# A tile of its own for the last phase's scaled x, and low halves of the second input projection read back from DRAM

## The chip, the core and the metric

The kernel runs on one core of one Trainium2 chip. The metric is the device time of one execution in microseconds (us). Three runs of the kernel before took 2285.0, 2285.44 and 2281.86 us; their median is 2285.0 us. One further execution was profiled, and the views quoted below come from it.

## What is computed

One layer of a hybrid decoder for two groups of requests that share the weights: a prompt of 1024 tokens and 8 sample tokens, model width 1024. Cut to its core:

```python
h = x + 0.5 * rmsnorm(swiglu(rmsnorm(x, n_ffn1_pre), gate1, up1, down1), n_ffn1_post)   # d_ff 2816
u = rmsnorm(h, n_mix_pre)
proj = u @ w_in                      # 1024 x 3328: 26 column tiles of 128
q, k, v = split(proj[..., :1536])    # group A: differential attention, 4 heads
pb = proj[..., 1536:]                # group B: RWKV-7, 8 heads of 64
ya = rmsnorm(attend(rope(q), rope(k), v), subln) * (1 - lam_init)
yb, state, shift = rwkv7_time_mix(pb, prev_shift, state0)
h = h + rmsnorm(concat(ya, yb) @ w_out, n_mix_post)
h = h + 0.5 * rmsnorm(swiglu(rmsnorm(h, n_ffn2_pre), gate2, up2, down2), n_ffn2_post)
```

The sample tokens attend over a paged cache of 512 past positions and carry a given RWKV state. Outputs are h for both groups, the new keys and values, the RWKV states and the last projected row.

## The kernel before

**Two halves, four phases.** Tokens lie along the free axis, features along the partitions. The 1032 tokens are cut into two halves: half 0 holds prompt tokens 0 to 511 and the 8 samples, half 1 prompt tokens 512 to 1023, as far as the first feed-forward goes. The feed-forward runs as phases 0 and 1 (first FFN of each half) and 2 and 3 (second FFN of each half; in phase 3 the samples lead). Each phase works on two column chunks, c = 0 and 1, of 256 or 264 tokens; phases 1 and 2 mostly use both at once (512 columns). Between them lie the input projection (`s_project`, half 0 and half 1), RWKV jobs (`s_job`), attention, and the output projection (`s_out`).

**Three matmuls for one.** Weights and activations in float32 are split into a high part, rounded to the fast matmul type, and a low part, the rest: `high = round(x)`, `low = x - high`. Each product is three matmuls that add up in PSUM: high x high, high x low, low x high (`mm3`). One weight tile of the input projection is 128 x 1024 numbers, 512 KB, for the high as for the low part. It gives 8 x 3 = 24 matmuls for each chunk.

**Where the low part comes from.** `split` (line 602) casts the raw tile to the high part on ScalarE, and then either subtracts on VectorE or GpSimd (`low`; `choose` takes the engine that is expected to be free first) or, where `kept` names a place in DRAM, reads the low part that an earlier use of the same weight wrote there. `first` marks the use that writes:

```python
if kept is not None and not first:
    self.aside(mine, kept)                   # read the low part from DRAM
...
    self.nc.scalar.copy(h[:, t], raw[:, t])
    if kept is None or first:
        self.low(l[:, t], raw[:, t], h[:, t].bitcast(F32))
if first and kept is not None:
    self.aside(kept, mine)                   # write it to DRAM
```

`LOWS` says for which weights this is done: before the change for the second FFN (`1`: DRAM tiles Ld, Lg) and the output projection (`"out"`: Lo). `K.Li`, the place for the input projection's 26 tiles, exists but is not used. `aside` issues these transfers on SyncE's DMA queue (SP), where nearly all other transfers are issued too, in order.

**The input projection.** `s_project` (line 1446) takes its 26 column tiles m in an order `ms`: 24, 25, 16, 12, 20, and so on; in half 1 the rest are 17, 13, 21, 18, 14, 22, 19, 15, 23, then 0 to 11. `s_linear` (line 655) loads each raw tile (two buffers in turn, lraw for even places and LT for odd ones in half 1), waits until the tile two places earlier has been used, and calls `split` into the weight tile of that earlier one. Half 0 works in units of 256 or 264 columns, half 1 from the third tile on in units of 512. Half 1's vector norm, `s_tail` of phase 1, comes just before its projection; its steps are called tail in the trace.

**Phase 3's input.** `s_pre(3)` (line 1214) scales the second residual by the row norm (`t = src * rstd`), eight tiles for each chunk, and splits each into the high and low matmul operands with `pair`: a ScalarE activation and a VectorE scalar_tensor_tensor, both of which read t. t lies in the pool tile `sq`, of which there are two, used in turn. The same two are used by the square sums at the end of a phase (`down(..., tail)` in `s_trunk`, through `square_sum`, line 755; in the trace trunk_sq, which are added to trunk_acc), by `s_tail`, and by `s_combine`. In the trace the scaled x is pre_sq, and the operands of phase 3 are pre_T.

**The tile dreg.** `dreg` is one large pool tile (128 x 4160 floats) with many tenants: activations of phase 1, the sample tokens' attention and RWKV step, half 1's attention (low parts of q and k, mix_dreg), and last, from `s_combine(3)` on, four sums of blocks of phase 3's input. `s_combine` forms such sums in phases 0 and 3 for a scheme that makes seven block products do for eight (`seven`), from the eleventh (phase 0) or fifth (phase 3) tile of the FFN's width on.

**A planned order.** The program does not run in the order in which it is written. Streams (generators with a label) hand operations to a planner, which keeps a model of the engines, orders the operations of every engine, and fixes that order in the program. It runs four times; from each run it works out the latest time at which each operation may start, and these due times are the priorities of the next one. `BIAS` (line 94) adds microseconds to the due times of a stream, named by label and count: a negative number makes its operations more urgent. `comb0` is `s_combine(0)`; `job03` is the fourth stream named job0, the second RWKV job of half 1 on buffer set 0 (`s_job`, i = 2). Any edit changes the plan as a whole.

Of the kernel before, what the change touches and what calls it, by code (L numbers as in the profile page):

```python
# [22 lines left out]
P = 128  # L23
# [34 lines left out]
def const_table():  # L58
# [11 lines left out]
    for g in range(4):  # L70
        for j in range(8):
# [8 lines left out]
W_DEC = 4160  # L80
# [10 lines left out]
MARG = 0  # L91
SLACK = 0.02
PASSES = 4
BIAS = {"trunk2": 300, "outn3": -60, "outb0": 30, "pre2": -3, "tail1": -30, "lora1": -10}
SHIFT = {}
SWAP = 0
MIX = 1
SQP = 0
RESAT = 3
GROUPS = {(0, 10): [[0, 1, 2], [3, 4], [5, 6, 7], [8, 9]], (3, 6): [[0, 1, 2], [3], [4, 5]],  # L100
          (0, 8): [[0, 1, 2], [3, 4], [5], [6, 7]], (0, 6): [[0, 1, 2], [3], [4, 5]], (3, 4): [[0, 1], [2, 3]], (3, 8): [[0, 1, 2], [3, 4], [5], [6, 7]]}
LOWS = (1, "out")
STARVE = 1
HUNGER = 0.1
RB = "dec"
# [107 lines left out]
class Kern:  # L213
# [99 lines left out]
    def put(self, eng, op, fn, a, k):  # L313
# [14 lines left out]
        if o.late is not None:  # L328
            o.late += BIAS.get(st.part, 0) + sum(d for a, b, d in self.shift.get(st.part, ()) if a <= o.key[1] < b)
        self.price(o, op, a, k, outs[0], ins)  # L330
# [468 lines left out]
    def stats(self, src, rb, tmp=("sqs", 1), **kw):  # L799

        for k in range(KT):
            if SQP:
                self.square_sum(rb, src[k], k, self.ps2()[:, :rb.shape[-1]], engines=("vector",))
            else:
                self.square_sum(rb, src[k], k, self.tmp(*tmp, rb.shape[-1]), **kw)
        self.rstd(rb)
# [64 lines left out]
    def s_weights(self):  # L871
# [3 lines left out]
        for ph in range(4):  # L875
# [4 lines left out]
            for n, (kind, f, m0) in enumerate(seq):  # L880
# [26 lines left out]
                kept = None  # L907
                if ph // 2 in LOWS and (kind == "down" or f < FAST[3 * (ph // 2)]):
                    kept = self.Ld[ph // 2][grp[0]:grp[-1] + 1, :, m0 * P:m0 * P + nm].rearrange("q p m -> p q m") if kind == "down" else \
# [304 lines left out]
    def s_pre(self, ph):  # L1214

        half = ph % 2
        if ph > 1:
            yield ("wait", ("outw", half))
        for c, (_, n) in enumerate(CHUNKS[ph]):
            yield ("wait", ("stage", ph, c))  # L1220
            if ph:
                yield ("wait", ("stats", ph, c))
            if c == 0:
                tiles = self.two(half)
                x = self.x[ph] = self.parts(ph, *tiles)
                self.xt[ph] = [t.rearrange("p (k t) -> p k t", t=520) for t in tiles]
            for k in range(KT):
                src = self.staged[c]
                if ph:

                    t = self.tmp("sq", 2, n) if ph == 3 else src[k]
                    self.either("tensor_tensor", t, src[k], self.own[c][2][:, :n], ALU.mult)
                    src = {k: t}
                for step in self.pair(k, src, f"n_ffn{1 + ph // 2}_pre", x[c]):
                    step()
                if k % 4 == 3:
                    yield
            self.signal(("x", ph, c))
            yield
        self.signal(("staged", ph))  # L1240
# [205 lines left out]
    def s_project(self, half):  # L1446

        nc = self.nc
        places = None
        for c in range(2):  # L1450
            yield ("wait", ("prb", half, c))
        if half:
            yield ("wait", ("outw", 0))
        else:
            yield ("wait", ("loaded", 1, "up", LEAD - 1, None))
            places = ("w0", "w1"), [("used", 1, kind, LEAD - 1, None) for kind in ("gate", "up")]

        job = [16, 12, 20]
        ms = [24, 25] + job
        ms = ms + [m + i for i in range(1, 4) for m in job] + list(range(12)) if half else \  # L1460
            ms + [m + 1 for m in job] + list(range(8)) + [m + i for i in range(2, 4) for m in job] + list(range(8, 12))

        def out(i, c, ps):
            o, n = SPANS[half][c]
            po = (self.rb if i % 2 else self.E)[:, o:o + n]
            nc.vector.tensor_tensor(po, ps, self.prb[:, o:o + n], ALU.mult)
            nc.sync.dma_start(self.PT[ms[i]][:, FIRST[half] + o:FIRST[half] + o + n], po)
            if c:
                self.signal(("done", half, ms[i]))

        units = [(i, c) for i in range(len(ms)) for c in ((2,) if half and i > 1 else range(2))]
        if half:
            units[:4] = [(0, 0), (1, 0), (0, 1), (1, 1)]
        yield from self.linear(("in", half), [self.column(self.I["w_in"], m) for m in ms], units, None, out, places,
                               [(self.Li[m], half == 0) for m in ms] if "in" in LOWS else None)
        self.signal(f"proj{half}")

    def s_out(self, half):
# [48 lines left out]
        if half:  # L1527
            yield ("wait", "states")
        yield from self.linear(("out", half), src, units, px, out, None, [(self.Lo[i % KT], half == 0) for i in range(len(src))] if "out" in LOWS else None)
        self.signal(("outw", half))  # L1530
# [1117 lines left out]
```

## Time and profile before

| | us |
|---|---|
| median of 3 runs | 2285.0 |
| lowest and highest run | 2281.86, 2285.44 |
| the profiled execution | 2287.04 |
| its span in the profile | 2284.6 |
| TensorE (PE) busy in the span | 2223.3 |
| VectorE (DVE), ScalarE (ACT), GpSimd (POOL) busy | 1537.3, 1098.8, 986.9 |
| moved by DMA | 343.15 MB |

The profiled execution took 2.04 us more than the median, and 2.4 us of its time lie outside the span. In a row of the timeline stand the start and the length of a run of like instructions, what they write and read, how many they are, and in brackets how long the engine was idle before and what released it. A matmul's length holds its pipelining, so the rate is read from a run of many. PEclk is TensorE's granted clock as a share of full speed. All operations are issued through one helper, so every row has line 320; the tiles' names tell them apart.

### The profile page before, as it was taken

How to read it: one execution, taken by the hardware profiler on the slowest of the kernel's cores; microseconds unless marked ns; L12 is line 12 of the kernel's file. 1: busy time of each engine (PE TensorE's matmuls, PEld its weight loads, DVE VectorE, ACT ScalarE, POOL GpSimd, SP SyncE). 2: the span in 40 equal slices, each digit the busy share in tenths (PEclk: the TensorE clock that was granted, in tenths of full speed). 3: DMA queues.
4: the chain of work that ended last, by engine and by line, in shares of the span. 5: the costliest groups of instructions: out<-in, count | busy, mean ns of one | idle time of the engine just before them, and what ended most of it. 6: DMA issues, size and time to landing. Idle time of an engine off the chain costs nothing.

```text
span 2284.6 us, 42790 instructions
## 1 busy us (share of the span) xinstructions
PE 2223.3 (97%) x15857; PEld 1981.1 (87%) x15857; DVE 1537.3 (67%) x3550; ACT 1098.8 (48%) x2256; POOL 986.9 (43%) x819
## 2 busy tenths in 40 slices
PE   7999999999999999999999999999999998999998
PEld 7999999799887778888877877777788888999998
DVE  5477888745766776568766466664676365778776
ACT  5443443635454366344562155543576555544444
POOL 3344555524333675456443124333434354544443
PEclk9999999999999999999999999999999999999999
DMA  6423334354433685655668753334636857434543
GB/s 203 135 84 94 110 93 131 102 148 140 113 107 104 184 244 174 211 177 151 178 205 213 193 146 111 106 86 115 199 112 172 276 165 240 148 114 126 148 139 112
DMA packets 476295, 343.15 MB, mean 150 GB/s; under 512 B 82457, under 2 KB 424061, under 8 KB 476088
## 3 DMA queue, kind: packets, MB, share of 16 engines
q1 hardware_dynamic: 475480, 338.82, 50.6%
q8 instruction: 125, 2.05, 0.4%
q0 software_dynamic: 320, 1.08, 0.1%
q14 instruction: 82, 0.67, 0.1%
q10 hardware_dynamic: 288, 0.52, 0.1%
HBM read 278.98 MB, written 61.38 MB: 149 GB/s over the span
## 4 chain that ended last, share of the span: by engine, by line
PE 77%; DVE 6%; ACT 6%; DMA 5%; issue 3%; POOL 2%; SPq 1%; DVEq 0%; ACTq 0%; POOLq 0%
PE trunk_m L320 44%; PE proj_m L320 12%; PE trunk_aux L320 7%; PE job_aux L320 4%; PE out_m L320 2%; PE outb_m L320 2%; PE attn_m L320 2%; PE attn_aux L320 1%; SPq L320 1%; ACT wts_w L320 1%; ACT mix_T L320 1%; DMA wts_raw<-in_ffn_gate_dram 1%; PE job_dec L320 1%; DMA lin_w<-Lo 1%; POOL wts_w L320 1%
## 5 line engine op out<-in xcount | busy, mean ns | idle before, releaser
L320 POOL TENSOR_TENSOR wts_w<-wts_raw,wts_w 128x1024 fp32r<-128x1024 f32 (+2 forms) x161 | 310.8, 1938 | 351.3 <-ACT wts_w L320 303.5
L320 PE MATMUL trunk_m<-trunk_xl,wts_w 128*128 128x256 f32 (+2 forms) x2700 | 456.5, 320 | 4.4 <-DVE trunk_xl L320 3.7
L320 PE MATMUL trunk_m<-pre_X,wts_w 128*128 128x512 f32 (+3 forms) x2400 | 439.9, 334 | 4.9 <-DVE pre_X L320 2.0
L320 PEld LDWEIGHTS trunk_m<-trunk_xl,wts_w 128*128 128x128 f32 x2700 | 381.4, 188 | 40.7 <-DVE trunk_xl L320 5.8
L320 PEld LDWEIGHTS trunk_m<-pre_X,wts_w 128*128 128x128 f32 x2400 | 351.3, 190 | 44.8 <-issue 3.7
L320 PE MATMUL trunk_m<-pre_T,wts_w 128*128 128x512 f32 (+3 forms) x1848 | 365.0, 348 | 6.5 <-DVE trunk_xl L320 2.7
L320 ACT CAST wts_w<-wts_raw 128x1024 fp32r<-128x1024 f32 (+2 forms) x293 | 244.2, 848 | 241.3 <-PE trunk_m L320 167.2
L320 PEld LDWEIGHTS trunk_m<-pre_T,wts_w 128*128 128x128 f32 x1848 | 288.1, 191 | 44.3 <-issue 3.9
L320 DVE TENSOR_TENSOR trunk_xl<-trunk_xl,trunk_m 128x256 f32<-128x256 f32 (+2 forms) x351 | 165.9, 491 | 57.7 <-PE trunk_m L320 56.4
L320 POOL TENSOR_TENSOR trunk_xl<-trunk_t,trunk_xl 128x512 fp32r<-128x512 f32 (+3 forms) x88 | 94.7, 1078 | 169.2 <-ACT trunk_xl L320 168.8
L320 PE MATMUL proj_m<-tail_xl,lin_w 128*128 128x256 f32 (+1 forms) x1248 | 166.5, 288 | 0.0
L320 PEld LDWEIGHTS proj_m<-tail_xl,lin_w 128*128 128x128 f32 x1248 | 153.9, 188 | 6.9 <-issue 5.1
L320 PE MATMUL proj_m<-tail_T,lin_w 128*128 128x512 f32 (+1 forms) x672 | 150.4, 380 | 3.0 <-DVE tail_T L320 1.9
L320 PEld LDWEIGHTS proj_m<-tail_T,lin_w 128*128 128x128 f32 x672 | 120.6, 188 | 31.0 <-DVE tail_T L320 3.0
L320 DVE TENSOR_TENSOR wts_w<-wts_raw,wts_w 128x1024 fp32r<-128x1024 f32 (+2 forms) x102 | 109.6, 1075 | 34.7 <-ACT wts_w L320 32.4
L320 POOL TENSOR_TENSOR lin_w<-lin_raw,lin_w 128x1024 fp32r<-128x1024 f32 x21 | 51.6, 2457 | 110.6 <-ACT lin_w L320 106.7
L320 ACT CAST wts_w<-wts_lraw 128x512 fp32r<-128x512 f32 x94 | 55.7, 619 | 72.0 <-DMA wts_lraw<-in_ffn_down_dram 35.0
L320 POOL TENSOR_TENSOR wts_w<-wts_lraw,wts_w 128x512 fp32r<-128x512 f32 x43 | 60.0, 1398 | 45.2 <-ACT wts_w L320 41.9
L320 PE MATMUL trunk_aux<-trunk_xl,wts_w 128*128 128x256 f32 (+1 forms) x516 | 71.7, 283 | 0.0
L320 DVE TENSOR_TENSOR trunk_t<-trunk_g,trunk_m 128x512 f32<-128x512 f32 (+2 forms) x75 | 41.9, 559 | 44.1 <-PE trunk_m L320 41.7
L320 PE MATMUL trunk_m<-comb_T,wts_w 128*128 128x260 f32 x540 | 69.4, 282 | 0.0
L320 ACT CAST wts_w<-wts_dec 128x512 fp32r<-128x512 f32 x30 | 17.6, 587 | 103.7 <-DVE wts_dec L320 102.0
(647 smaller groups left out, 4263.8 us busy)
## 6 DMA issues: line engine op xcount, KB each, us to landing
wts_raw<-in_ffn_gate_dram SPq DMA_DIRECT2D x88, 512.0 KB
wts_raw<-in_ffn_up_dram SPq DMA_DIRECT2D x58, 512.0 KB
wts_raw<-in_ffn_down_dram SPq DMA_DIRECT2D x56, 384.0 KB
wts_raw<-in_ffn_down_dram SPq DMA_DIRECT2D x29, 512.0 KB
lin_raw<-in_w_in_dram SPq DMA_DIRECT2D x26, 512.0 KB
wts_w<-Ld SPq DMA_DIRECT2D x22, 512.0 KB
mix_T<-PT SPq DMA_DIRECT2D x37, 256.0 KB
Ld<-wts_w SPq DMA_DIRECT2D x24, 384.0 KB
```

Source lines behind the costliest of these rows:

```text
L320: o = Op(eng, lambda: fn(*a, **k), st)
```

## The change

Four edits. In phase 3 the scaled x gets 16 separate slices of `dreg`, a new tenant of it, in place of the two `sq` tiles in turn. The input projection's low parts go through DRAM where m is odd (`ODD = 1`; 13 of 26 tiles): half 0 subtracts as before and writes the low part to `Li`, half 1 reads it and does not subtract. An even m is left as it was, in both halves. Two entries are added to `BIAS`: comb0 -60 and job03 +60. The edit of `stats` and `SQP` alone does nothing, since `SQP` is empty as it was 0.

```diff
-BIAS = {"trunk2": 300, "outn3": -60, "outb0": 30, "pre2": -3, "tail1": -30, "lora1": -10}
+BIAS = {"trunk2": 300, "outn3": -60, "outb0": 30, "pre2": -3, "tail1": -30, "lora1": -10, "comb0": -60, "job03": 60}
-SQP = 0
+SQP = ()
+ODD = 1
-LOWS = (1, "out")
+LOWS = (1, "in", "out")
@@ def stats
-            if SQP:
+            if SQP and tmp[0] in SQP:
@@ def s_pre
                 self.xt[ph] = [t.rearrange("p (k t) -> p k t", t=520) for t in tiles]
+                scaled = self.T(self.pool, [P, W_DEC], "dreg") if ph == 3 else None
...
-                    t = self.tmp("sq", 2, n) if ph == 3 else src[k]
+                    t = scaled[:, 2112 * c + n * k:2112 * c + n * k + n] if ph == 3 else src[k]
@@ def s_project
-                               [(self.Li[m], half == 0) for m in ms] if "in" in LOWS else None)
+                               [(self.Li[m], half == 0) if not ODD or m % 2 else () for m in ms] if "in" in LOWS else None)
```

## The prediction

> **What bounds the kernel now.** I read the page first, then the busy time by stage, then what TensorE waited for in the stages that the change touches, and last the timeline around those waits.
>
> ```profile
> span 2284.6 us, 42790 instructions
> PE 2223.3 (97%) x15857; PEld 1981.1 (87%) x15857; DVE 1537.3 (67%) x3550; ACT 1098.8 (48%) x2256; POOL 986.9 (43%) x819
> ```
>
> TensorE is busy for 97% of the span. The change leaves every matmul in place, so it can only act on the 2284.6 - 2223.3 = 61.3 us in which TensorE waits, and on the clock that is lost around waits. The stages (span; busy time of PE, PEld, DVE, ACT, POOL; granted clock, DMA share, GB/s) are: half 0's projection, the passage from phase 1 to half 1's projection, that projection, half 1's output projection, and the passage from phase 2 to 3:
>
> ```profile
> 456.00:680.00 224.00, 222.70 (x2046) 205.11 (x2046) 135.95 (x443) 99.09 (x183) 72.96 (x57) 1.00 0.44 128
> 1120.00:1185.00 65.00, 58.77 (x372) 52.44 (x372) 51.81 (x92) 42.56 (x78) 33.94 (x39) 0.97 0.72 216
> 1185.00:1322.00 137.00, 137.00 (x598) 110.02 (x598) 74.57 (x106) 34.51 (x39) 29.71 (x14) 1.00 0.76 197
> 1760.00:1855.00 95.00, 92.98 (x597) 83.22 (x596) 36.41 (x66) 47.40 (x81) 33.83 (x37) 1.00 0.82 258
> 1855.00:1910.00 55.00, 49.10 (x348) 44.77 (x347) 41.89 (x74) 35.22 (x66) 30.57 (x33) 1.00 0.43 129
> ```
>
> Where the low parts are to be read, 1185 to 1322, TensorE has no idle time at all. Time is lost in the two passages: 65 - 58.77 = 6.2 us and 55 - 49.10 = 5.9 us. From 1855 to 1960 TensorE waited for (total, times, longest):
>
> ```profile
> PE rows_cb L320 <- ACT rows_X L320: 2.2, 2, 1.5
> PE last_aux L320 <- ACT trunk_xl L320: 2.1, 1, 2.1
> PE trunk_m L320 <- ACT trunk_sq L320: 1.9, 1, 1.9
> PE trunk_m L320 <- DVE trunk_xl L320: 0.8, 1, 0.8
> ```
>
> **Part 1: the scaled x.** No operation is added or removed; 16 multiplications write other slices. What goes is the turn-taking on two tiles, with phase 2's closing square sums in the same queue for them. Rows of VectorE, ScalarE, GpSimd and TensorE:
>
> ```profile
> 1885.33 0.75 DVE L320 TENSOR_TENSOR trunk_xl<-trunk_xl,trunk_m 128x256 f32<-128x256 f32 x2
> 1897.50 0.43 DVE L320 TENSOR_TENSOR trunk_acc<-trunk_acc,trunk_sq 128x256 f32<-128x256 f32 x1 [0.62 <-POOL trunk_acc L320]
> ...
> 1889.86 0.51 ACT L320 ACTIVATE pre_T<-pre_sq,setup_cols 128x256 fp32r<-128x256 f32 x1 [0.31 <-POOL pre_sq L320]
> 1890.27 0.40 ACT L320 ACTIVATE trunk_sq<-trunk_xl 128x256 f32<-128x256 f32 x1
> ...
> 1890.75 2.40 POOL L320 TENSOR_TENSOR trunk_acc<-trunk_acc,trunk_sq 128x256 f32<-128x256 f32 x3 [0.93 <-ACT trunk_sq L320]
> ...
> 1884.70 0.59 ACT L320 COPY rows_X<-rows_cb 128x512 f32<-128x512 f32 x1
> 1885.34 0.66 PE L320 MATMUL rows_cb<-init_ident,outb_T 128*128 128x128 f32 x4 [0.68 <-ACT rows_X L320]
> ...
> 1898.40 5.02 PE L320 MATMUL trunk_m<-trunk_xl,wts_w 128*128 128x256 f32 x35 [0.82 <-DVE trunk_xl L320]
> 1908.01 6.09 PE L320 MATMUL trunk_m<-pre_T,wts_w 128*128 128x264 f32 x48 [1.88 <-ACT trunk_sq L320]
> ```
>
> The second result of phase 2's close was there at 1885.33 + 0.75 = 1886.1, yet its square began at 1890.27, right behind the last step that reads the scaled x: 4.2 us late. GpSimd's additions start late with it, VectorE waits at 1897.50 for them, the eviction queued behind that addition comes late, and TensorE waits 0.82 us at 1898.40. Meanwhile phase 3's operands, for whose sake the squares stood back, are first used at 1908.01, some 17 us after they were done at 1890.4. With places of their own the scaled x need no longer be read before the squares can be written. I take as gained the 0.82 us, the 1.88 us at 1908.01 (ScalarE works off squares there) and the 0.68 us at 1885.34, where a copy to the rows is queued among the scaled x's steps: **-3.4 us**. Bounds: nothing, if ScalarE's order alone held the square back, and -3.4 - 2.1 = -5.5 us, if the wait for trunk_xl in the list goes too. The new tenant of dreg makes nobody wait: what held it before is half 1's attention, over when the output projection starts at about 1760, and what follows on it, the block sums, waits for all of the scaled x already.
>
> **Part 2: 13 subtractions less, 13 reads more.** Tile 25, second in the order, is odd. Its subtraction lies on the chain of waits (start, length) before half 1's projection:
>
> ```profile
> 1131.53 0.18 DVE lin_w L320
> 1131.71 0.94 issue
> 1132.65 1.26 DVE trunk_xl L320 x3
> 1133.92 0.74 POOL trunk_xl L320
> 1134.67 4.23 DMA tail_hres<-res
> ...
> 1131.49 3.10 PE L320 MATMUL trunk_m<-pre_X,wts_w 128*128 128x256 f32 x24
> 1153.04 4.05 PE L320 MATMUL trunk_m<-pre_X,wts_w 128*128 128x256 f32 x21
> ```
>
> Without it the chain moves up by 0.18 + 0.94 = 1.1 us. The waits in this passage also cost clock: 21 matmuls at 4.05 / 21 = 193 ns against 129 ns (3.10 / 24) earlier, 21 x 0.064 = 1.3 us, with 0.97 granted over the stage. I take both: **-2.5 us**, bounds 0 and -2.5. By the Trainium skill (TensorE: Matmul & The Clock Gate, What's actually happening) the clock falls after an idle window of about 3.4 us. No single wait here is that long and the clock fell all the same, so the trace doesn't bear this out in that form. By the rule the short waits would have cost no clock, and this term would be -1.1 us.
>
> The other 12 odd tiles are among the 24 wide ones. In the stage 1185 to 1322:
>
> ```profile
> L320 PE MATMUL proj_m<-tail_T,lin_w 128*128 128x512 f32 x575 | 135.1, 395 | 0.0
> L320 DVE TENSOR_TENSOR lin_w<-lin_LT,lin_w 128x1024 fp32r<-128x1024 f32 x9 | 11.5, 1274 | 0.8 <-ACT lin_w L320 0.8
> L320 POOL TENSOR_TENSOR lin_w<-lin_lraw,lin_w 128x1024 fp32r<-128x1024 f32 x6 | 14.5, 2418 | 56.4 <-ACT lin_w L320 41.0 <-DMA mix_T<-PT 12.5 <-DMA decb_dreg<-Dd 2.9
> ```
>
> 12 subtractions at 1.27 us (VectorE) to 2.42 us (GpSimd) are 15 to 29 us of engine time, and TensorE waited 0.0 us for any of it: this is worth **0**. The price is on the other side. A read can be issued once the tile two places back is used; until its low part is needed TensorE has one tile, 24 x 135.1 / 575 = 5.64 us, and the two matmuls on the high part, 0.47 us: 6.1 us of cover. The like reads of the output projection:
>
> ```profile
> L320 PE MATMUL outb_m<-outb_T,lin_w 128*128 128x264 f32 (+1 forms) x384 | 48.9, 284 | 2.0 <-DMA lin_w<-Lo 1.9
> ...
> 1812.85 7.93 DMA lin_w<-Lo
> 1823.73 5.62 DMA lin_w<-Lo
> ```
>
> Those that set the end took 5.62 to 7.93 us. Per read that is between no wait and 7.93 - 6.1 = 1.8 us, for 12 between 0 and 22 us. I take what 16 such reads cost there, 1.9 us, or 0.12 each: **+1.5 us** for 13. A tile there lasts only 24 x 48.9 / 384 = 3.1 us, with other matmuls put in between; here it lasts longer. While such a read waits on SP for its slot, everything behind it waits as well: the projection's results on their way to PT, and the loads of the sample tokens' RWKV step; TensorE waits for neither in this stage. The reads bring 12 x 0.524 MB in 137 us, 46 GB/s, on 197; with the share per GB/s of the output projection's stage (0.82 at 258) the DMA share rises from 0.76 to about 0.91. The Trainium skill (DMA: Bandwidth & Descriptors, Latency and other measured facts) puts an access to DRAM at 0.2 us on average and 2 us at high load; that speaks against the middle I chose, and for reads near the 7.93 us. This is a rival below.
>
> Half 0 writes 13 low parts, 30 GB/s more on 128. The slot is needed again two tiles later, and the write starts before its tile is used, so it has two tiles' time. The nearest row is the first output projection, which writes 8 low parts in shorter tiles:
>
> ```profile
> L320 PE MATMUL out_m<-out_X,lin_w 128*128 128x256 f32 x384 | 46.6, 281 | 0.0
> ```
>
> TensorE waited 0.0 us there: **0**. Were the cover gone, one write late by the 1.8 us above, once, would be the price.
>
> **Part 3: the two biases.** Phase 0's block sums are ready long before they are used; rows of VectorE and TensorE:
>
> ```profile
> 161.97 0.96 DVE L320 TENSOR_TENSOR comb_T<-comb_sq,comb_T 128x260 fp32r<-128x260 f32 x1
> ...
> 195.28 1.60 PE L320 MATMUL trunk_m<-comb_dreg,wts_w 128*128 128x260 f32 x12
> ```
>
> That is 32 us of slack, so comb0 earlier by up to 60 us is worth **0**; it might cost the 1 us that one displaced subtraction lasts. job03 acts between 1322 and 1600, where TensorE waited for jobs:
>
> ```profile
> PE job_aux L320 <- ACT mix_T L320: 2.3, 7, 0.6
> PE job_aux L320 <- DVE mix_T L320: 1.2, 4, 0.5
> PE job_aux L320 <- DVE job_hres L320: 1.1, 1, 1.1
> ```
>
> Together 4.6 us. One of four jobs is moved, and against its partner on the other buffer set, so that one's short matmuls can fall into the other's gaps. Bounds are all of it gone and as much again, -4.6 and +4.6. I take a quarter, **-1.2 us**.
>
> **The sum:** -3.4 - 2.5 + 1.5 - 1.2 = -5.6 us. Against the profiled execution's 2287.04 us that is 2281.4; this execution lay 2.04 us above the median of the runs, 2285.0, and on the scale of the runs the forecast is **2279.4 us**.
>
> **The rivals.** (a) *The reads come late and TensorE becomes bound by them.* Speaking for it: no idle time in the stage now, and a share of 0.91 where 0.82 gave landings up to 7.93 us. Against it: in the outputs' stage TensorE lost only 1.9 us. It decides from a landing of 6.1 us on. At half of the way to 7.93, 0.9 us a read, 12 reads cost 11 us in place of 1.5: -5.6 + 9.5 = +3.9, 2289 us; at the full 1.8 us, 22 us, 2300 us. I put it at 2291. (b) *More goes than I count.* Part 1 at its bound (-5.5), the jobs at theirs (-4.6), tile 25 in full and the reads hidden: -5.5 - 4.6 - 2.5 = -12.6, 2272 us. For it: the passages hold 12.1 us of waits. Against it: other waits are often next in line. (c) *It is hidden anyway.* The square was late because ScalarE was full, the chain before the projection is met by its load of the residual, and only the +1.5 us of the reads remains, or nothing: 2285 to 2286.5. For it: the 17 us of slack show that phase 3's input as such is not on the path. Against it: the 0.82 us follow step by step from the late square. (d) *The new plan as a whole* moves waits that no part touches; of the 61.3 us in the span I can't say which, so this widens the range only.
>
> **How the numbers follow.** Chances: forecast 0.46, with its own range 2276 to 2283; (a) 0.25; (b) 0.19; (c) 0.10. About 0.2%, 4.6 us, is what a measurement of this kernel can tell from no change: faster means under 2280.4, slower over 2289.6. Of the forecast some three quarters (0.36) and all of (b) are faster: 0.55. Of (a) most and a little of (d) are slower: 0.24. The rest, 0.21, is the same. The range runs from 2266 (b, with half as much again for the plan) to 2295 (a, between its half and its full price).
>
> **What would show it.** Part 1 is right if phase 2's second square starts within about 1 us of its input and TensorE's waits between 1880 and 1910 shrink by 3 us; wrong if the square still follows the last scaled x. Part 2 is right if half 1's projection runs 575 wide matmuls in about 135 us with waits for Li under 2 us in all, and VectorE's step before the tail's chain is gone; a list of waits of proj_m for lin_w<-Li of 5 us or more would be rival (a). comb0 is right if the first block product starts without a wait. The forecast fails if the reads land later than 6.1 us, or if waits arise in stages that no part touches.

## The result and the profile after

The changed kernel took 2297.2 us (median of 4 runs, 2292.7 to 2299.8) and the kernel before, on the same chip, 2283.4 us (4 runs). The ratio is 1.006, with a 95% interval of 1.0048 to 1.0073: some 13.8 us slower. The forecast was 2279.4 us with a range to 2295.

The profiled execution of the changed kernel took 2292.67 us, 4.55 under its median, and that of the kernel before 2287.04 us, 3.61 over the 2283.43 here. Of the 13.8 us the two profiles thus show only 5.6. The profiled execution of the changed kernel was the fastest of its four and had the highest granted clock of them (0.994; the others 0.993, 0.989 and 0.991); the place of the rest of the 13.8 us is in no trace. First the head of the page after:

```profile
span 2290.9 us, 42826 instructions
PE 2226.4 (97%) x15857; PEld 1983.4 (87%) x15857; DVE 1530.6 (67%) x3548; ACT 1097.0 (48%) x2256; POOL 960.1 (42%) x806
```

TensorE runs the same 15857 matmuls. It waits 2290.9 - 2226.4 = 64.5 us in place of 61.3, and its matmuls take 3.1 us longer in all. The busy time by stage, after (span; PE, PEld, DVE, ACT, POOL; granted clock, DMA share, GB/s):

```profile
456.00:680.00 224.00, 220.72 (x2041) 203.72 (x2040) 138.71 (x437) 98.73 (x183) 72.37 (x57) 1.00 0.52 157
1120.00:1185.00 65.00, 58.95 (x408) 54.48 (x407) 46.65 (x96) 41.70 (x79) 33.35 (x41) 0.95 0.66 203
1185.00:1322.00 137.00, 134.99 (x586) 107.31 (x585) 66.82 (x104) 37.35 (x46) 19.32 (x11) 1.00 0.97 248
1855.00:1910.00 55.00, 51.40 (x359) 47.69 (x358) 37.86 (x62) 32.27 (x66) 30.93 (x36) 0.97 0.38 115
```

The DMA share where the low parts are read rose from 0.76 to 0.97 (I had forecast 0.91), and TensorE now idles 2.0 us there. Half 0's projection, where they are written, idles 3.3 us in place of 1.3. The passage from phase 2 to 3 idles 3.6 us in place of 5.9. None of these is 13.8 us. The largest single loss is in a stage that I had not quoted, because no part of the change touches it: the close of phase 1. The same view, first before, then after:

```profile
1082.00:1120.00 38.00, 37.80 (x256) 34.42 (x254) 29.18 (x72) 16.63 (x30) 17.82 (x11) 1.00 0.46 133
```

```profile
1082.00:1120.00 38.00, 34.16 (x184) 29.24 (x183) 27.49 (x62) 13.58 (x22) 12.65 (x8) 0.91 0.39 109
```

TensorE's idle time goes from 0.2 to 3.8 us and the granted clock from 1.00 to 0.91, another 0.09 x 38 = 3.4 us. Other stages win some of it back: from 1322 to 1760 TensorE idles 6.9 us in place of 11.0. The timeline of VectorE, SP and TensorE in phase 1's close, after:

```profile
1084.13 5.18 SPq L2527 DMA_DIRECT2D dec_dreg<-in_cache_v_dram  x3
1084.66 4.29 DVE L321 SCALAR_TENSOR_TENSOR dec_dreg<-dec_dreg 128x128 f32<-128x128 f32 x8 [0.56 <-DMA dec_dreg<-in_cache_v_dram]
1088.88 1.27 DVE L321 TENSOR_TENSOR trunk_xl<-trunk_xl,trunk_m 128x512 f32<-128x512 f32 x2
1089.61 3.05 PE L321 MATMUL trunk_m<-trunk_xl,wts_w 128*128 128x512 f32 x9 [2.85 <-DVE trunk_xl L321]
```

In the new order eight steps of the sample tokens' attention (dec_dreg) stand ahead of two evictions of the trunk on VectorE's queue. They take 4.29 us, and TensorE waits 2.85 us for the evictions. In the kernel before the evictions stand one by one between such steps, and TensorE waits for none of them by more than 0.2 us from 1082 to 1120:

```profile
1084.72 2.98 DVE L320 SCALAR_TENSOR_TENSOR dec_dreg<-dec_dreg 128x128 f32<-128x128 f32 x8
1087.63 0.67 DVE L320 TENSOR_TENSOR trunk_xl<-trunk_xl,trunk_m 128x512 f32<-128x512 f32 x1
```

In the changed kernel the clock halves at about 1091, some 1.4 us after TensorE went on. Three stretches of 7 us (columns as above):

```profile
1084.00:1091.00 7.00, 4.15 (x18) 3.03 (x18) 6.44 (x15) 1.06 (x1) 2.39 (x1) 1.00 0.63 179
1091.00:1098.00 7.00, 7.00 (x23) 5.80 (x22) 5.09 (x13) 1.05 (x1) 2.37 (x1) 0.51 0.44 135
1098.00:1105.00 7.00, 7.00 (x32) 5.67 (x31) 3.07 (x7) 2.74 (x5) 2.18 (x1) 1.00 0.35 101
```

TensorE is busy for all of the second stretch, so with the wait of 2.85 us about as much again was lost in clock, 0.49 x 7 = 3.4 us. The Trainium skill (TensorE: Matmul & The Clock Gate, What's actually happening) has the clock halved after an idle window of some 3.4 us that runs free of the kernel. The halving agrees; a wait of 2.85 us, shorter than the window, was enough here.

### The profile page after: what moved, and what is told of

Read it like the earlier page. It is cut to its first block, busy times and chain, and to the rows that moved or that the text cites. A ratio compares the mean times of both kernels' runs of the same rounds, so it can differ in the third digit from the quotient of the medians.

```text
span 2290.9 us, 42826 instructions
## 1 busy us (share of the span) xinstructions
PE 2226.4 (97%) x15857; PEld 1983.4 (87%) x15857; DVE 1530.6 (67%) x3548; ACT 1097.0 (48%) x2256; POOL 960.1 (42%) x806
## 5 line engine op out<-in xcount | busy, mean ns | idle before, releaser
L321 PE MATMUL trunk_m<-trunk_xl,wts_w 128*128 128x256 f32 (+2 forms) x2700 | 461.7, 321 | 9.0 <-DVE trunk_xl L321 5.8
L321 POOL TENSOR_TENSOR trunk_xl<-trunk_t,trunk_xl 128x260 fp32r<-128x260 f32 (+3 forms) x81 | 83.7, 1037 | 144.3 <-ACT trunk_xl L321 144.0
L321 PEld LDWEIGHTS trunk_m<-comb_T,wts_w 128*128 128x128 f32 x540 | 66.7, 188 | 0.0
```

What stands on the lines that cost most here:

```text
L321: o = Op(eng, lambda: fn(*a, **k), st)
```

## The experiments

Times are compared with runs of the kernel before on the same chip (medians 2280.6 to 2281.3 us in the experiments); microseconds are the ratio's surplus times 2281. "Order of work" here means what the planner decides: the sequence on every engine, and for some steps whether VectorE or GpSimd does them. "Nudged" is an order that the planner made after one of its own numbers was altered by 1 to 5%. o_place and o_writes, at 1.0000 and 1.0004, show that holding an order costs nothing by itself.

| kernel | order of work | operations | ratio (95%) | us |
|---|---|---|---|---|
| after | its own | all of the change | 1.006 (1.0048-1.0073) | +13.7 |
| e_place | its own | scaled x in dreg | 1.0014 (1.0005-1.0023) | +3 |
| e_low | its own | writes and reads of Li | 1.0084 (1.0068-1.0099) | +19 |
| e_bias | its own | those of before | 1.0035 (1.0022-1.0048) | +8 |
| e_no_bias | its own | scaled x, writes, reads | 1.0051 (1.0038-1.0064) | +12 |
| o_place | that of before | scaled x in dreg | 1.0000 (0.999-1.0009) | 0 |
| o_writes | that of before | writes only | 1.0004 (0.9995-1.0013) | +1 |
| o_no25 | that of before | 12 writes and reads | 1.006 (1.0046-1.0073) | +14 |
| o_low | that of before | 13 writes and reads | 1.0077 (1.0061-1.0093) | +18 |
| o_all | that of before | scaled x, writes, reads | 1.008 (1.0066-1.0093) | +18 |
| p_low | that of e_low | those of before | 1.0058 (1.0045-1.0071) | +13 |
| p_a | that of after | scaled x, no Li | 1.0067 (1.0054-1.008) | +15 |
| n_slack | nudged | those of before | 1.003 (1.0019-1.0041) | +7 |
| n_tail1 | nudged | those of before | 1.0118 (1.0103-1.0133) | +27 |
| n_land | nudged | those of before | 1.0123 (1.0107-1.0138) | +28 |
| a_tail1 | nudged | all of the change | 1.0102 (1.0086-1.0118) | +23 |
| a_land | nudged | all of the change | 1.0127 (1.0111-1.0142) | +29 |

**Each part alone.** My first theory (A) was that the new order of work as a whole had moved waits into stages that no part touches; the rival (B), that the reads cost the time where they are made. The three parts were made alone in the kernel before:

```diff
+                scaled = self.T(self.pool, [P, W_DEC], "dreg") if ph == 3 else None
-                    t = self.tmp("sq", 2, n) if ph == 3 else src[k]
+                    t = scaled[:, 2112 * c + n * k:2112 * c + n * k + n] if ph == 3 else src[k]
```

> The kernel before with the first part alone: the last phase's scaled x in dreg, no reads of Li, no biases. Theory A (the 13.8 us are lost where the new order of work as a whole moved waits, above all in phase 1's close, 1082 to 1120): the part itself saves up to 3.4 us in phase 2's close; if this part's new order alone brings the loss at 1082 to 1120 back (7 us there), the time is 2287 to 2292, otherwise 2279 to 2283. Theory B (the reads of Li and the DMA share of 0.97 cost the time): no reads here, so 2279 to 2283.

```diff
-LOWS = (1, "out")
+LOWS = (1, "in", "out")
...
+                               [(self.Li[m], half == 0) if not ODD or m % 2 else () for m in ms] if "in" in LOWS else None)
```

> The kernel before with the second part alone: 13 low parts written and read back. Theory B (reads): all of the loss is here, 2290 to 2298, with waits of proj_m for lin_w<-Li or lost time of 3 us and more in 1185 to 1322. Theory A (new order of work): the reads cost no more than 3.5 us where they are made; the time is 2283 to 2288 unless this part's own new order moves a wait elsewhere, which the windows outside 1120 to 1322 would show.

```diff
-BIAS = {"trunk2": 300, "outn3": -60, "outb0": 30, "pre2": -3, "tail1": -30, "lora1": -10}
+BIAS = {"trunk2": 300, "outn3": -60, "outb0": 30, "pre2": -3, "tail1": -30, "lora1": -10, "comb0": -60, "job03": 60}
```

> The kernel before with the two biases alone. Theory A: the biases are what moves work between stages, so a good part of the loss is here, 2288 to 2296, in windows that neither the scaled x nor the reads touch. Theory B: 2281 to 2285, no change that can be told.

The fourth is the changed kernel with the line BIAS of before:

> The changed kernel without the two biases: scaled x in dreg and the reads. Theory A: the waits in 1082 to 1120 and the halved clock there are gone, 2280 to 2288. Theory B: the reads are still there, 2290 to 2298. If the parts add up, its difference to the kernel before is the sum of the differences of the scaled x alone and the reads alone; if it misses that sum by over 4 us, the order of the whole decides and not the parts.

The scaled x alone cost 3 us (its order is that of before up to about 1850 us) and the biases, which change no operation at all, 8 us; the reads alone cost 19, more than the whole change. The parts don't add up: the scaled x and the reads together cost 12, where 3 + 19 = 22 would be the sum. By my own condition the order decides, but e_low's 19 us leave room for (B), and e_low cannot tell the reads from the order that was made around them.

**Order and operations taken apart.** In the next kernels the planner decides the order with one set of operations, and another set is issued. A planned instruction can be left out (skip), and one that the planner doesn't know can be issued with another one, or 0.2 us after its planned end (ride):

```diff
+            self.nc.scalar.copy(h, raw)
+            if not first:
+                self.ops[-1].ride = None, "sync", lambda: sync.dma_start(mine, kept)
+            self.low(l, raw, h.bitcast(F32))
+            if first:
+                self.ops[-1].ride = 0.2, "sync", lambda: sync.dma_start(kept, mine)
+            else:
+                self.ops[-1].skip = True
```

> The order of work of the kernel before, held fixed on every engine, with the operations of the second part: 13 low parts written behind their subtractions in half 0, 13 read in half 1 in place of the subtractions. Theory A (the order decides): 2281 to 2286, like the kernel before. Theory B (the writes and reads themselves cost the time, whatever the order): 2291 or more, near the 19 us that the second part alone cost.

For the scaled x the sequence of all planned operations was recorded with the old place and then issued in that sequence with the new one:

```diff
+                key, e = self.take[0][len(self.order)]
+                o, = [st.q[e][0] for st in self.streams if st.key == key[0] and st.q[e] and st.q[e][0].key == key]
```

> The order of work of the kernel before, held fixed, with the operations of the second part and the scaled x in dreg. Theory A: 2278 to 2286; what the scaled x's own place saves without a new order is the difference to the run with the second part alone in this order (my prediction took 3.4 us). Theory B: 2291 or more.

The other way round, planned with the reads and issued with the subtractions:

```diff
+                self.aside(mine, kept)
+                self.last_aside.skip = True
+            self.nc.scalar.copy(h, raw)
...
+                self.ops[-1].ride = 0.2, e, lambda: less(e)
```

> The order of work that the second part alone makes, held fixed, but with the operations of the kernel before: no writes and reads of Li, all subtractions (13 in half 1 put back behind their casts, in turn on GpSimd and VectorE). Theory A: 2293 to 2301, as slow as with the reads. Theory B: 2280 to 2286.

> The changed kernel's order of work, held fixed, with its scaled x in dreg, but without the writes and reads of Li; the 13 subtractions are put back. Theory A: 2291 to 2299, like the changed kernel. Theory B: 2280 to 2286.

Both theories were met, and each only by half. The writes and reads cost 18 us in the order of before (B). The orders made around the reads cost 13 to 15 us without a single read (A). In the changed kernel's order it makes no difference that can be told whether the low parts are read (13.7 us with the reads, 15.3 without); in the order of the second part alone the reads cost some 6 us more (19 and 13). The order of the changed kernel with the scaled x on the two old tiles was not tried, since that order counts on the place of their own.

The planner did not know of the subtractions that were put back, so they might themselves be what costs p_a its 15 us. Its trace speaks against that. Rows of p_a:

```profile
1082.00:1120.00 38.00, 33.82 (x173) 28.62 (x172) 27.09 (x61) 12.53 (x21) 12.25 (x7) 0.87 0.38 109
1185.00:1322.00 137.00, 137.00 (x599) 109.93 (x598) 78.86 (x111) 39.52 (x49) 35.30 (x18) 1.00 0.82 210
```

In half 1's projection, where 12 of the 13 subtractions are, TensorE has no idle time. The loss in phase 1's close, which lies ahead of all of them, is there as in the changed kernel: the same eight steps of 4.29 us stand ahead of the same two evictions, and TensorE waits 3.17 us. So this loss comes with the order and not with the reads. The 13th subtraction, tile 25's, lies in the passage from 1120 to 1185, where p_a idles 7.8 us and the changed kernel 6.05, at the same granted clock of 0.95; it can have cost some 1.7 us there.

What the reads cost in the order of before, 1185 to 1322, and what TensorE waited for from 1100 to 1330, o_low:

```profile
1185.00:1322.00 137.00, 129.75 (x551) 102.65 (x550) 62.27 (x99) 33.83 (x38) 17.63 (x10) 0.98 0.93 239
```

```profile
PE proj_m L329 <- DMA lin_w<-Li: 7.2, 4, 4.0
PE proj_m L329 <- DVE tail_T L329: 4.5, 1, 4.5
```

The longest of the four waits for Li, in the timeline of o_low:

```profile
1232.43 4.53 SPq L329 DMA_DIRECT2D decb_dreg<-Dd  x5
...
1237.62 1.05 ACT L329 CAST lin_w<-lin_LT 128x1024 fp32r<-128x1024 f32 x1 [3.37 <-PE proj_m L329]
1237.67 0.58 SPq L329 DMA_DIRECT2D decb_dreg<-Dd  x1
1238.35 0.60 SPq L329 DMA_DIRECT2D lin_lraw<-in_w_in_dram  x1
1239.30 1.37 SPq L329 DMA_DIRECT2D decb_dreg<-Dd  x2
...
1240.77 1.15 SPq L673 DMA_DIRECT2D lin_w<-Li  x1
...
1247.56 5.06 PE L329 MATMUL proj_m<-tail_T,lin_w 128*128 128x512 f32 x11 [3.99 <-DMA lin_w<-Li]
```

The slot was free at 1237.62, when the cast into it began. The read is issued 3.15 us later, because SP has the sample tokens' loads (decb_dreg) and the load of a raw tile ahead of it, and TensorE goes on 6.8 us after the issue. My 6.1 us of cover were about right (3.15 + 6.8 - 3.99 = 6.0) and so were the landings of 5.6 to 7.9; what I had left out is the 3 us in SP's queue. Here too the clock was halved for some 7 us, from the last part of the wait on, so that 5.44 us of the low clock fell on work:

```profile
1246.00:1253.00 7.00, 5.44 (x13) 4.37 (x14) 2.68 (x4) 0.63 (x1) 0.00 (x0) 0.52 1.12 304
```

When the planner knows of the reads it finds better places for them, though not equally good ones: TensorE waits 2.7 us for Li in e_no_bias, 3.1 in a_land and 4.7 in a_tail1, and less in two others (waits for Li, second part alone and the changed kernel; the second row is from 1185 to 1322):

```profile
PE proj_m L321 <- DMA lin_w<-Li: 2.6, 2, 2.1
```

```profile
PE proj_m L321 <- DMA lin_w<-Li: 1.9, 2, 1.0
```

**Writes, and tile 25.** Two more kernels in the order of before, one without the reads, one with tile 25 subtracted:

```diff
-            if not first:
-                self.ops[-1].ride = None, "sync", lambda: sync.dma_start(mine, kept)
...
-            else:
-                self.ops[-1].skip = True
```

> The order of work of the kernel before, held fixed, and only the 13 writes of low parts in half 0; nothing is read and all subtractions stay. My step put the writes at 0. Theory B1 (the reads cost it): 2280 to 2285, and 456 to 680 loses no more than before. Theory B2 (the writes delay what SP loads and stores behind them for the jobs): 2285 to 2290, with waits of the job's products for mix_T or job_hres in 456 to 680.

```diff
-                               [(self.Li[m], half == 0, PLANNED["low"] != MADE["low"]) if m % 2 else () for m in ms]
+                               [(self.Li[m], half == 0, PLANNED["low"] != MADE["low"]) if m % 2 and m != 25 else () for m in ms]
```

> As the second part in the order of before, but tile 25 (the one in the passage before half 1's projection) is subtracted as before; 12 are written and read. If the read of tile 25 delays the residual's load (7.8 us to landing in place of 4.2) and with it the first products, the wait of 4.5 us for tail_T goes back to about 1 and the time falls by 3 to 5 us against the 13 reads in this order (2297). If that wait has another cause, the time stays at 2295 to 2300.

The writes cost 1 us with an interval that holds nothing (-1.1 to +3.0 us), as B1 has it. But TensorE idles 3.2 us from 456 to 680 in place of 1.3, with a wait of 1.5 us for mix_T, which is the sign of B2; a cost of up to 3 us is not excluded. The time of o_no25 is 4 us below that of o_low, but the intervals overlap; the traces tell it more clearly. The residual's load and what waits for it, with 13 reads (o_low), then with 12 (o_no25):

```profile
1132.83 2.99 SPq L329 DMA_DIRECT2D tail_hres<-res  x2
1140.66 0.42 DVE L329 TENSOR_TENSOR trunk_xl<-trunk_xl,tail_hres 128x256 f32<-128x256 f32 x1 [4.03 <-DMA tail_hres<-res]
```

```profile
1135.51 1.74 SPq L329 DMA_DIRECT2D tail_hres<-res  x2
1139.42 0.42 DVE L329 TENSOR_TENSOR trunk_xl<-trunk_xl,tail_hres 128x256 f32<-128x256 f32 x1
1141.46 0.62 PE L329 MATMUL proj_m<-tail_T,lin_w 128*128 128x256 f32 x3 [0.60 <-DVE tail_T L329]
```

With the read ahead of it in the same queue, the load lands 7.8 us after its issue (1132.83 to 1140.66) in place of 3.9 (1135.51 to 1139.42), so that it comes later although it was issued earlier. TensorE waits for tail_T on VectorE once, for 4.5 us, with the read of tile 25, and five times, for 1.6 us in all, without it.

**Is it the orders around the reads, or any other order?** That the biases alone cost 8 us suggested a third theory (A'): the order of before is an unusually good one. Its rival (A''): only the orders made around the reads are bad. Two kernels keep every operation of before and tell the planner one slightly different number. Some steps change their engine with the plan: n_tail1 has 3558 operations on VectorE and 811 on GpSimd, before 3550 and 819. Its order is that of before up to about 460 us.

```diff
-BIAS = {"trunk2": 300, "outn3": -60, "outb0": 30, "pre2": -3, "tail1": -30, "lora1": -10}
+BIAS = {"trunk2": 300, "outn3": -60, "outb0": 30, "pre2": -3, "tail1": -29, "lora1": -10}
```

> The kernel before with one number of the planner changed by one (tail1: -30 to -29): every operation is the same, the order is another from the first phase on. Theory A' (the order of before is an unusually good one, and almost any other one costs several us): 2286 to 2296. Theory A'' (only the orders made around the reads are bad): 2279 to 2285.

```diff
-LAND = 2.0
+LAND = 2.02
```

> The kernel before with the planner's allowance for the landing of a transfer at 2.02 in place of 2.0: every operation is the same, the order is another. Theory A': 2286 to 2296. Theory A'': 2279 to 2285.

Both were slower by twice as much as the whole change, 27 and 28 us, beyond what even (A') expected, and (A'') falls. Part of it is again in the passage to phase 3. Rows of 1855 to 1960 of before, n_tail1 and n_land:

```profile
1855.00:1960.00 105.00, 97.02 (x734) 92.45 (x733) 68.85 (x128) 64.83 (x123) 53.75 (x62) 0.98 0.66 201
```

```profile
1855.00:1960.00 105.00, 89.46 (x635) 85.26 (x634) 58.45 (x109) 57.91 (x102) 46.14 (x58) 0.90 0.53 160
```

```profile
1855.00:1960.00 105.00, 93.31 (x673) 87.50 (x672) 59.64 (x111) 61.11 (x108) 49.24 (x59) 0.95 0.61 185
```

e_bias and n_slack lose in this passage too: TensorE is busy for 92.64 and 93.63 us of it, at a granted clock of 0.93 in both.

And TensorE's largest group of waits over the whole span, before, after, n_tail1, n_land:

```profile
PE trunk_m L320 <- DVE trunk_xl L320: 6.3, 10, 2.2
```

```profile
PE trunk_m L321 <- DVE trunk_xl L321: 10.2, 10, 2.9
```

```profile
PE trunk_m L320 <- DVE trunk_xl L320: 15.7, 13, 6.4
```

```profile
PE trunk_m L320 <- DVE trunk_xl L320: 14.3, 17, 3.2
```

It is the same kind of wait that grows in all three, the one for the trunk's evictions on VectorE, from 6.3 to 10.2, 15.7 and 14.3 us. It is no measure of the loss, though: in a_land, the slowest of all below, it is 8.0 us.

**The same nudges on the changed kernel, a third one, and the scaled x by itself.** The two nudges were then made in the changed kernel, a third (SLACK 0.02 to 0.019, which, but for a few steps, alters the order from about 1400 us on) in the kernel before, and the scaled x's place was taken alone in the order of before:

> The changed kernel with the planner's allowance for a landing at 2.02 in place of 2.0; its operations are the same. The same small change to the kernel before cost 26 us. Theory A' (any order that was not picked out is slow, with the reads or without): 2300 to 2315. Rival C (orders made around the reads are steadily about 14 us slow): 2293 to 2300.

> The changed kernel with tail1 at -29 in place of -30. The same small change to the kernel before cost 25 us. Theory A': 2300 to 2315; if the reads and the scaled x's place are worth something by themselves, these two runs are on average faster than the two of the kernel before at 2306 and 2308. Rival C: 2293 to 2300.

> The kernel before with the planner's slack at 0.019 in place of 0.02; its operations are the same, and the order is the same up to about the middle of the kernel. Theory A': part of the 25 us that the orders changed from the start on cost, 2285 to 2300. Theory A'': 2279 to 2285.

> The order of the kernel before, held fixed, with the scaled x in dreg and nothing else. My step: the closing squares of phase 2 need no longer wait for the last reader of the scaled x, -3.4 us, 2278. Theory A: with every queue in the order of before the squares still come behind those readers on ScalarE, so nothing moves, 2281 to 2283.

The nudged pairs average 1.0121 with the operations of before and 1.0115 with those of the changed kernel: over these two orders the change's operations are worth 0.0006, about 1 us, within the uncertainty of each. The pairs themselves differ in direction: with tail1 the changed kernel is 3.6 us faster than the kernel before, with the landing 0.9 us slower. Rival C falls, since the changed kernel's own order is 10 to 15 us better than its nudged neighbours. The scaled x by itself is worth nothing that can be measured, and o_all and o_low, 18 us each, say the same. Its square and TensorE's waits in o_place:

```profile
1880.69 0.75 DVE L329 TENSOR_TENSOR trunk_xl<-trunk_xl,trunk_m 128x256 f32<-128x256 f32 x2
1884.70 0.51 ACT L329 ACTIVATE pre_T<-pre_dreg,setup_cols 128x256 fp32r<-128x256 f32 x1
1885.11 0.41 ACT L329 ACTIVATE trunk_sq<-trunk_xl 128x256 f32<-128x256 f32 x1
...
1893.61 5.02 PE L329 MATMUL trunk_m<-trunk_xl,wts_w 128*128 128x256 f32 x35 [0.82 <-DVE trunk_xl L329]
1903.21 7.59 PE L329 MATMUL trunk_m<-pre_T,wts_w 128*128 128x264 f32 x48 [1.88 <-ACT trunk_sq L329]
```

The square still begins right behind the last reader of the scaled x, 1885.11 - 1881.44 = 3.7 us after its input, and the waits of 0.82 and 1.88 us are there to the hundredth. ScalarE's order holds it, not the tile. One thing differs: the 48 matmuls behind the wait of 1.88 us take 7.59 us here and took 6.09 in the kernel before, because the granted clock from 1900 to 1915 is 0.89 (before, 1905 to 1920: 1.00). In the changed kernel, whose order is another, the squares do follow their inputs:

```profile
1892.67 0.42 DVE L321 TENSOR_TENSOR trunk_xl<-trunk_xl,trunk_m 128x256 f32<-128x256 f32 x1 [0.54 <-PE trunk_m L321]
1893.74 0.42 ACT L321 ACTIVATE trunk_sq<-trunk_xl 128x256 f32<-128x256 f32 x1
```

There the 1.88 us for trunk_sq are gone, but the first matmul on phase 3's operands now waits 1.83 us for trunk_xl, the next in line. TensorE's waits in the same passage (1855 to 1960):

```profile
PE trunk_m L321 <- DVE trunk_xl L321: 2.1, 2, 1.8
PE trunk_m L321 <- DVE trunk_g L321: 2.1, 1, 2.1
PE trunk_m L321 <- DVE wts_w L321: 1.2, 1, 1.2
```

## Why the prediction was wrong

The step that failed is the one that I did not price: rival (d), "the new plan as a whole moves waits that no part touches ... this widens the range only". It is the largest effect here. An order made anew cost 7 to 28 us with the operations of before (n_slack, n_tail1, n_land; 8 for the biases), so in none of four tries was its effect near zero, and in none a gain. In the changed kernel's own case, its order without a single read or write of Li costs 15 us (p_a), about as much as the change as a whole (13.7). The order of before is the exception: all ten kernels whose operations are issued in an order planned for them, the changed one among them, were slower, by 3 to 29 us (the two least, e_place and n_slack, keep most of the order of before). My sum took each part's effect as if all else stayed in its place.

- **Part 1, -3.4 us:** wrong as a term. With the order held it is 0.0 (interval -2.3 to +2.1 us); its lower bound, "nothing, if ScalarE's order alone held the square back", is what happened. In the changed kernel the mechanism came about as I described it (square about 0.7 us after its input), but the passage lost in clock (0.97) and in new waits part of what it saved.
- **Tile 25, -2.5 us:** wrong in sign in the order of before, where its read costs some 4 us (18 - 14; the intervals overlap). The 1.1 us of the chain did come free (the residual's load is issued at 1132.83 in place of 1134.67), but the next step of the chain that I had quoted, the residual's load, took 3.9 us more with the read ahead of it in the same queue than without it. I had rival (c)'s "met by its load of the residual" as hidden, not as dearer.
- **The 12 reads, +1.5 us:** too small in the order of before, where 12 cost 14 - 1 = 13 us (between half and full price of rival (a)); in the changed kernel TensorE waits 1.9 us for them, near my figure, and in four more orders that the planner made for them 2.6 to 4.7. Landings and cover were right, the place in SP's queue was missing, and with the longest wait clock was lost as well. That rival (a)'s full price, 2300, lies near the 2297 measured is luck: it is the price of reads that come late, and the changed kernel's order is as slow without them.
- **The writes, 0:** right within what the time can tell, 1 us (o_writes, -1.1 to +3.0), though TensorE idles 1.9 us more in their stage.
- **comb0 and job03, -1.2 us:** wrong; alone they cost 8 us, and the trace shows a loss in the passage from phase 2 to 3, in which neither of the two streams works.
- **The test that I named**, "waits in stages that no part touches", is what first pointed to it, in phase 1's close. The range ended 2 us short; its upper end was built from the reads' price alone, with nothing for a plan that is worse as a whole.

What stays open is which of the moved steps makes an order good: the runs show some of the places where orders lose, not a rule for it, and how the order of before was come by is not on record. Two nudges are also few for an average over orders.

## What to carry to other kernels

Where a planner or a compiler orders the work anew after each edit, first measure how far a nudge without meaning moves the time (here 7 to 28 us), and hold the order fixed to learn what an edit is worth by itself. That worth is one for the order held: the reads cost 18 us with the writes in the order of before and some 6 in one planned for them. A kernel whose order is better than its neighbours, as here against ten others, is likely to lose by an edit at first, whatever the edit is worth. A read that spares a computation has to be costed with the queue in which it is issued and with the loads behind it, not by its landing time alone.

## What the runs showed of the hardware

A wait of TensorE can cost more than its length. With the wait of 2.85 us in the changed kernel (to 1089.61) the granted clock was 0.51 from 1091 to 1098, all of it busy: 3.4 us more. With that of 3.99 us in o_low (to 1247.56) it was 0.52 from 1246 to 1253, of which TensorE worked for 5.44 us: 0.48 x 5.44 = 2.6 us more. The same matmuls run either way, so this stands in the page as busy time and not as idle time: 3.1 of the 6.3 us between the two profiled spans are busy time.

The length of the wait alone does not tell the price. The wait for the two evictions in phase 1's close comes in five kernels whose order was planned with the reads. At 2.46 us (p_low) the granted clock from 1080 to 1110 stayed at 1.00, at 2.56 (e_low) and 2.62 (e_no_bias) it was 0.94, at 2.85 (the changed kernel) 0.89, and at 3.17 (p_a) 0.83, that is from nothing to 0.17 x 30 = 5.1 us. And behind the wait of 1.88 us before phase 3's first product the clock stayed full in the kernel before and fell in o_place.

For some orders the clock is the larger part of the loss. In p_low TensorE idles 2296.6 - 2233.8 = 62.8 us, only 1.5 more than before, while its 15857 matmuls take 2233.8 us in place of 2223.3. The mean granted clock of the runs of e_low, n_tail1 and p_a is 0.990 and of p_low 0.991, and that of the kernel before 0.995 to 0.996 beside them; 0.005 x 2290 gives some 11 us, an estimate from these figures and an upper one, since part of the low clock falls on waits. That the waits bring the low clock is read from where it stands in the traces; no run changed the one without the other.
